# A mixed-attention block on one core: the order of its interleaved part written by a model of the engines

## The chip, the cores and the metric

The kernel runs on one core of a Trainium2 chip. The metric is the device time of one execution in microseconds. The core has a matmul engine (TensorE, PE in the profile, with its weight loads as PEld), three engines for the other arithmetic (VectorE = DVE, ScalarE = ACT, GpSimd = POOL), and a queue for transfers (SyncE = SP).

## The reference

One layer over 512 tokens of width 1024. A normed and modulated `h` is projected by `w_in` to some 8,450 columns, which feed three branches of eight heads of width 64 each, and three gates. Cut to what matters:

```
h = rms_norm(x) * norm1_g * (1 + sc1) + sh1        # sc, sh, gt from silu(c) @ w_ada
y_fox  = softmax attention with a decay, causal, q and k rms-normed per head
y_hgrn = gated linear recurrence in chunks of 64
y_rwkv = delta-rule recurrence in chunks of 64, then a group norm
merged = sigmoid(g0) * (y_fox @ w_branch[0]) + sigmoid(g1) * (y_hgrn @ w_branch[1]) + sigmoid(g2) * (y_rwkv @ w_branch[2])
x = x + gt1 * (merged @ w_out)
h = rms_norm(x) * norm2_g * (1 + sc2) + sh2
u = conv3(h @ w_up);  x = x + gt2 * ((silu(u_gate) * u_val) @ w_down)
```

All is fp32. A large product is made as three matmuls in a faster fp32 form, from a high and a low part of each operand (`mm3`).

## The kernel before

The kernel has four stages: a start that loads and norms `x` (to 47 us), an interleaved part (47 to about 707 us), the output projection with the second norm, and the feed-forward half (from about 760 us), which is one long run of large matmuls.

In the interleaved part the kernel's Python writes the instructions of seven streams, each a generator: `rwkv_b`, `rwkv_a`, `hgrn` and the attention stream `fox` (each over four pairs of heads), `prep`, `ada_stream` (the rest of the adaLN product, on VectorE), and `big`. `big` is the list of large jobs: the projections from `w_in`, the gates, and the merges with `w_branch`; it writes groups of three large matmuls and asks for the weights of later jobs in `ahead()`, as long as fewer than four halves of weights stand behind the job under way. A half is 256 KB; it comes into one of three `raw` buffers (`load`, line 338) and is split into `whi` and `wlo` (lines 330 and 331), with six buffers each. A weight half thus waits for TensorE to be done with an older one.

The other streams work on a pair of heads in many short steps: small matmuls on tiles of the array (64x64, 32x32, 128x64 and so on), transposes and sums over a head (whole 128x128, and 128x32), with VectorE, ScalarE and GpSimd work between. The matmul results of these streams rotate through five accumulators (tag `br`, `PSB`), those of `big` through three (tag `mm`, `PSM`). Nearly all other tiles share one ring of 62 buffers (`T2`).

A stream gives control back with `yield`. `run` keeps a clock of TensorE alone (`clk`, advanced by `mm` and `transpose`); a step that yields x is taken up again after 0.9x + 1.65 us of that clock, and of the streams that are due, the first in the list goes. `big` is last, so large matmuls fill what the others leave. `need` waits for a result of another stream, which `post` puts up with a guessed latency. The compiler then builds the queue of each engine from what is written, the earlier written first among those that it holds to be ready.

Of the kernel before, what the change touches and what calls it, by code (L numbers as in the profile page):

```python
# [40 lines left out]

@with_exitstack
def block_kernel(ctx: ExitStack, tc: tile.TileContext, I, out, dbg=None, upto=99):
    nc = tc.nc
    sync, v, s, g, pe = nc.sync, nc.vector, nc.scalar, nc.gpsimd, nc.tensor
# [18 lines left out]
    LAT = (0.9, 1.65)  # L64
# [15 lines left out]
    clk = [0.0]  # L80

    def mm(o, lhsT, rhs, start=True, stop=True):
        n = rhs.free_size() if hasattr(rhs, "free_size") else math.prod(rhs.shape[1:])
        if rhs.dtype == F32R:
            clk[0] += n / 2400
        else:
            half = (0.5 if lhsT.shape[0] <= 64 else 1.0) * (0.25 if math.prod(lhsT.shape[1:]) <= 32 else 1.0)
            clk[0] += half * max(0.17, n / 600)
        return pe.matmul(o, lhsT=lhsT, rhs=rhs, start=start, stop=stop)  # L89

    def transpose(o, i, idn):
        clk[0] += 0.11 if i.shape[0] > 64 else 0.07
        pe.transpose(o, i, idn)
# [15 lines left out]
    def run(streams):  # L109

        live = [[gen, 0.0, False] for gen in streams]
        while live:
            done = False
            for st in live:
                if st[1] > clk[0] + 1e-9:
                    continue
                c0, n0 = clk[0], len(avail)
                try:
                    lat = next(st[0])
                except StopIteration:  # L120
                    live.remove(st)
                    done = True
                    break
                if lat is None and c0 == clk[0] and n0 == len(avail):
                    continue
                lat = lat or 0.0
                st[1] = clk[0] + (lat * LAT[0] + LAT[1] if lat else 0.0)
                done = True
                break
            if not done:  # L130
                later = [st[1] for st in live if st[1] > clk[0] + 1e-9]
                assert later, "streams wait for each other"
                clk[0] = min(later)

    def PSM():
        return psm.tile([P, 512], F32, tag="mm", name=nm("mm"))

    def PSB():
        return psb.tile([P, 512], F32, tag="br", name=nm("br"))
# [186 lines left out]
    def split(raw, shape, leng):  # L326
        hi = wp.tile(list(shape), F32R, tag="whi", bufs=WB[1], name=nm("whi"))
        lo = wp.tile(list(shape), F32R, tag="wlo", bufs=WB[2], name=nm("wlo"))
# [5 lines left out]
    def load(src, r0, nr, c0, ncol):  # L334
        nld[0] += 1
        sh = [P, nr // P, ncol]
        raw = wp.tile(sh, F32, tag="raw", bufs=WB[0], name=nm("raw"))
# [111 lines left out]
    def head_sums(sqs, sums=None):  # L449
# [8 lines left out]
        yield 0.6  # L458
# [24 lines left out]
    def hgrn(gi):  # L483
# [10 lines left out]
        yield 3.5  # L494
# [9 lines left out]
        yield 1.5  # L504

        fa = T2("fta")
        for li, m in enumerate(LEVELS):
# [28 lines left out]
            yield 2.0  # L536
# [16 lines left out]
        yield 1.8  # L553
# [12 lines left out]
        yield 3.0  # L566
# [7 lines left out]
        yield 1.0  # L574
# [3 lines left out]
        yield 1.0  # L578
        on = T2("on", [P, 8, 64])
        v.tensor_tensor(out=on, in0=as3(ps, 64), in1=bc(ss, 2, [P, 8, 64]), op=ALU.mult)  # L580
        yield 1.0
# [4 lines left out]
        yield 0.8  # L586
        dump("yh", y, lambda d: d[gi * P:(gi + 1) * P, :])
        post(("y", 1, gi), y, 0.0)

    def hgrn_evac(n, gi, ps):  # L590
# [13 lines left out]
        post((n, gi), t, 1.5)  # L604
# [9 lines left out]
    def fox_decay():  # L614
# [8 lines left out]
        yield 6.0  # L623
# [6 lines left out]
        yield 1.5  # L630
        s.activation(nz, nz, AF.Exp)
        s.activation(nz, nz, AF.Ln, bias=1.0)
        yield 2.0
# [14 lines left out]
        yield 0.0  # L648

    def fox_evac(n, gi, ps):  # L650
        raw = T2(n)
        s.activation(raw, ps, AF.Copy)
        post((n, gi), raw, 1.0)

    def fox(gi):
# [5 lines left out]
        yield 1.2  # L661
# [13 lines left out]
        yield 5.0  # L675
        for qi in range(2):
            rnx = head_spread(rn[:, qi, :])
            yield 0.8
# [14 lines left out]
            yield 0.0  # L693
# [6 lines left out]
        yield 3.0  # L700
        y = T2("yf")
        for tt in range(4):
# [14 lines left out]
            yield 1.0  # L717
# [5 lines left out]
            yield 1.0  # L723
# [4 lines left out]
            yield 1.0  # L728
# [10 lines left out]
            yield 1.0  # L739
# [6 lines left out]
            yield 0.0  # L746
# [696 lines left out]
```

## Time and profile before

| | |
|---|---|
| median of 3 runs | 1132.48 us (1131.71 to 1133.53) |
| profiled execution | 1132.57 us, span 1130.7 us |
| TensorE busy | 1072.1 us, 95% of the span |
| VectorE, ScalarE, GpSimd busy | 677.5, 525.8, 277.1 us |
| mean granted TensorE clock | 0.985 of 2.4 GHz |

The span is what lies between the first and the last instruction. Busy times come from the profiler's records; matmuls overlap in the array, so their mean durations (0.39 us for a large one) are longer than their spacing (0.23 us).

### The profile page before, as it was taken

Reading aid. Unit: us, or ns where it says so; the run is one execution under the profiler, and the core shown is the slowest. Engines: PE = TensorE matmul, PEld = TensorE weight load, DVE = VectorE, ACT = ScalarE, POOL = GpSimd, SP = SyncE. Lnnn points to the kernel's source line nnn. Section 1 sums busy time; section 2 is a strip of 40 time slices with the busy share of each in tenths; the row PEclk is TensorE's granted clock in tenths of the full one; section 3 lists DMA queues with packets and bytes.
Section 4 is the critical chain, followed back from the end, with each engine's and each line's share of the span. In section 5 each row is a group of like instructions: output and inputs, shape, how many; then the busy total and the mean of one; then the engine's idle time right before and its main releaser. Section 6 shows DMA issues by size and latency. Waiting matters only on the chain. (4 is left out here: it accounts for less than half of the span.)

```text
span 1130.7 us, 19788 instructions
## 1 busy us (share of the span) xinstructions
PE 1072.1 (95%) x7617; PEld 856.0 (76%) x7617; DVE 677.5 (60%) x1369; ACT 525.8 (47%) x967; POOL 277.1 (25%) x274
## 2 busy tenths in 40 slices
PE   4988999899999999989999999899999999999998
PEld 2567777778777777767778887678888888888886
DVE  2567666777688776786744617446666656651124
ACT  3475475366556647386444235124444444442220
POOL 4015421414341341340022514332011110101100
PEclk9999999899999999999999999899999999999999
DMA  9623233214422441344335365202333333332232
GB/s 323 199 72 86 72 91 95 65 51 134 103 57 73 117 114 49 87 117 127 92 106 175 104 184 170 66 2 71 100 96 100 93 96 101 99 97 95 93 103 84
DMA packets 175476, 117.55 MB, mean 104 GB/s; under 512 B 25360, under 2 KB 151350, under 8 KB 175382
## 3 DMA queue, kind: packets, MB, share of 16 engines
q1 hardware_dynamic: 173696, 116.13, 35.6%
q8 instruction: 60, 0.98, 0.4%
q10 hardware_dynamic: 1238, 0.12, 0.1%
q14 instruction: 34, 0.28, 0.1%
q0 software_dynamic: 448, 0.03, 0.0%
HBM read 112.49 MB, written 3.77 MB: 103 GB/s over the span
## 5 line engine op out<-in xcount | busy, mean ns | idle before, releaser
L330 ACT ACTIVATE whi<-raw 128x512 fp32r<-128x512 f32 x282 | 176.6, 630 | 342.8 <-PE mm L89 227.8
L331 DVE TENSOR_TENSOR wlo<-raw,whi 128x512 fp32r<-128x512 f32 x212 | 151.5, 715 | 152.1 <-ACT whi L330 151.7
L331 POOL TENSOR_TENSOR wlo<-raw,whi 128x512 fp32r<-128x512 f32 x70 | 94.0, 1342 | 516.9 <-ACT whi L330 503.7
L89 PE MATMUL mm<-hhi,whi 128*128 128x512 f32 x504 | 205.2, 407 | 2.8 <-ACT gt L1095 2.5
L89 PE MATMUL mm<-hhi,wlo 128*128 128x512 f32 x504 | 198.8, 394 | 0.0
L89 PE MATMUL mm<-hlo,whi 128*128 128x512 f32 x504 | 198.6, 394 | 0.0
L89 PE MATMUL mm<-h2hlo,whi 128*128 128x512 f32 (+1 forms) x376 | 141.5, 377 | 1.2 <-POOL h2hlo L1293 1.2
L89 PE MATMUL mm<-h2hhi,whi 128*128 128x512 f32 (+1 forms) x376 | 141.3, 376 | 0.0
L89 PE MATMUL mm<-h2hhi,wlo 128*128 128x512 f32 (+1 forms) x376 | 141.2, 376 | 0.0
L89 PEld LDWEIGHTS mm<-hhi,whi 128*128 128x128 f32 x504 | 95.5, 189 | 25.0 <-ACT gt L1095 2.9
L89 PEld LDWEIGHTS mm<-hhi,wlo 128*128 128x128 f32 x504 | 95.2, 189 | 20.9 <-issue 0.4
L89 PEld LDWEIGHTS mm<-hlo,whi 128*128 128x128 f32 x504 | 95.6, 190 | 18.2 <-issue 0.8
L89 PEld LDWEIGHTS mm<-h2hlo,whi 128*128 128x128 f32 x376 | 70.7, 188 | 14.8 <-POOL h2hlo L1293 2.0
L89 PEld LDWEIGHTS mm<-h2hhi,wlo 128*128 128x128 f32 x376 | 70.7, 188 | 12.9
L89 PEld LDWEIGHTS mm<-h2hhi,whi 128*128 128x128 f32 x376 | 70.7, 188 | 12.8
L1351 DVE SCALAR_TENSOR_TENSOR u<-mm,cw,u 128x511 f32<-128x511 f32 x44 | 32.9, 747 | 54.6 <-ACT u L1350 54.6
L1171 DVE SCALAR_TENSOR_TENSOR adac<-ada,cs,adac 128x512 f32<-128x512 f32 x56 | 45.7, 816 | 10.7 <-DMA ada<-in_w_ada_dram 10.6
L89 PE MATMUL br<-wlo,ahi 128*128 128x512 f32 x110 | 42.8, 389 | 0.0
L89 PE MATMUL br<-whi,alo 128*128 128x512 f32 x110 | 42.8, 389 | 0.0
L89 PE MATMUL br<-whi,ahi 128*128 128x512 f32 x110 | 42.8, 389 | 0.0
L89 PE MATMUL mm<-yhi,whi 128*128 128x512 f32 x96 | 38.3, 399 | 0.0
L89 PE MATMUL mm<-yhi,wlo 128*128 128x512 f32 x96 | 37.5, 390 | 0.0
(387 smaller groups left out, 1936.9 us busy)
## 6 DMA issues: line engine op xcount, KB each, us to landing
raw<-in_w_in_dram SPq DMA_DIRECT2D x126, 256.0 KB
ada<-in_w_ada_dram SPq DMA_DIRECT2D x96, 256.0 KB
raw<-in_w_up_dram SPq DMA_DIRECT2D x88, 256.0 KB
raw<-in_w_down_dram SPq DMA_DIRECT2D x44, 256.0 KB
raw<-in_w_branch_dram SPq DMA_DIRECT2D x24, 256.0 KB
wo<-in_w_out_dram SPq DMA_DIRECT2D x16, 256.0 KB
x<-in_x_dram SPq DMA_DIRECT2D x8, 256.0 KB
mg<-in_x_dram SPq DMA_DIRECT2D x8, 256.0 KB
```

The costliest lines, as they stand in the source:

```text
L89: return pe.matmul(o, lhsT=lhsT, rhs=rhs, start=start, stop=stop)
L330: s.activation(hi, raw, AF.Copy)
L331: (g if leng == "g" else v).tensor_tensor(out=lo, in0=raw, in1=hi.bitcast(F32), op=ALU.subtract)
L1171: v.scalar_tensor_tensor(out=acc, in0=raws[n], scalar=cs[:, k:k + 1], in1=acc, op0=ALU.mult, op1=ALU.add)
L1351: v.scalar_tensor_tensor(out=u[:, 1:], in0=ps[:, :511], scalar=cw[:, 1, jj:jj + 1], in1=u[:, 1:], op0=ALU.mult, op1=ALU.add)
```

## The change

`run` no longer goes by a clock of TensorE and fixed latencies. A new class `Plan` keeps a model of all engines while the Python writes: each engine's operations with an estimated cost, when each tile is ready and when it was last used, the slots of accumulators and of weights, the transfers, and in which tile shape TensorE works. `v`, `s`, `g` and `sync` become `Planned` objects, which pass every call on and enter it in the model. A step now says of what kind its next work is: `"f"` (free: goes first whenever ready), `"s"` (small tiles), `"b"` (large). Small steps are held while whole matmuls run, until 3 us have passed since the last return to whole ones or since the step was ready. The constants were not changed elsewhere: `WB`, `NP2` and the loop `ahead()` are as before. Two steps are cut: `split2` of `rk` and of the adaLN sums is now followed by a `yield` before the matmuls that read it. One more `yield` stands before the `BK` transposes.

```diff
+SEM, DRAIN, CHANGE, ENTER = 0.08, 0.2, 0.11, 0.1
+START, HOLD, SLACK = 47.0, 3.0, 0.1
+class Plan:
...
+    def place(self, engine, at, took):
+        b = self.busy.setdefault(engine, [])
...
+        for i, (x, y) in enumerate(b):
+            if at + took <= x:
+                b.insert(i, (at, at + took))
+                return at + took
+            at = max(at, y)
+        b.append((at, at + took))
+        return at + took
+
+    def other(self, engine, op, outs, ins):
+        n = outs[0].free_size()
+        psum = any("PSUM" in str(a.space) or "PS" == str(a.space).split(".")[-1] for a in (*outs, *ins))
+        if engine == "ACT":
+            took = 0.2 + 0.85e-3 * n + (0.19 if len(outs) > 1 else 0.0)
+        elif engine == "POOL":
+            took = 0.3 + 2.2e-3 * n if n > 16 else 0.2 + 0.18 * n
+        else:
+            one = len([a for a in ins if a.free_size() > 8]) < 2 and not psum
+            took = 0.17 + (0.6e-3 if one else 1.15e-3) * n + (0.08 if psum else 0.0)
+        end = self.place(engine, max(self.when((*outs, *ins)), self.slot.get(outs[0].tensor.name, 0.0)) + SEM, took)
+        self.done(outs, ins, end)
+        self.seg = max(self.seg, end)
+
+    def transfer(self, o, i):
...
+        self.sp = max(self.sp, self.when((o, i)), self.slot.get(o.tensor.name, 0.0)) + 0.1
+        self.dma = max(self.sp, self.dma) + 4 * n / 250e3
+        self.done([o], [i], self.dma + 2.0)
+
+    def matmul(self, o, w, x, turn=False):
...
+        at = max(self.pe, self.when((w, x)) + SEM, self.slot.get(o.tensor.name, 0.0) + SEM)
+        if mode != self.mode:
+            at += CHANGE + (ENTER if mode == WHOLE else 0.0)
+            self.mode = mode
+        self.pe = at + took
+        self.done([o], [w, x], self.pe + DRAIN)
...
-    def need(*keys):
+    def need(*keys, kind="f"):
         for k in keys:
             while k not in avail:
                 yield None
-        t = max(avail[k][0] for k in keys) - clk[0]
-        if t > 0:
-            yield t
+        yield (kind, max(avail[k][0] for k in keys))
         return [avail[k][1] for k in keys]
-    def post(key, val, lat=0.0):
-        avail[key] = (clk[0] + lat, val)
+    def post(key, val):
+        avail[key] = (plan.seg, val)
     def run(streams):
-        live = [[gen, 0.0, False] for gen in streams]
...
-                lat = lat or 0.0
-                st[1] = clk[0] + (lat * LAT[0] + LAT[1] if lat else 0.0)
...
+        plan.begin(START)
+        live = [dict(gen=gen, at=plan.pe, kind="f", n=-1, big=i == len(streams) - 1) for i, gen in enumerate(streams)]
+        left = plan.pe
         while live:
+            t = plan.pe
+            ready = [st for st in live if st["n"] != len(avail) and st["at"] <= t + SLACK]
+            small = [st for st in ready if st["kind"] == "s"]
+            free = [st for st in ready if st["kind"] == "f" and not st["big"]]
+            big = [st for st in ready if st["big"]]
+            if plan.whole() and big and small and t - left < HOLD and t - min(st["at"] for st in small) < HOLD:
+                small = []
+            pick = free or small or big
+            if not pick:
...
+                plan.pe = max(plan.pe, min(st["at"] for st in later))
+                continue
...
+            if plan.whole() and not was:
+                left = plan.pe
...
+            elif isinstance(y, float):
+                st["kind"], st["at"] = "f", plan.pe + y
+            elif y == "b":
+                st["kind"], st["at"] = "b", plan.wready
+            else:
+                st["kind"], st["at"] = y, plan.seg
...
@@ def hgrn
-        yield 3.5
+        yield "f"
...
-            yield 2.0
+            yield "s" if m < 32 else "f"
...
@@ def rwkv_a
+        yield "f"
+        parts = split2(rk)
+        yield "f"
         psk = PSB()
-        for i, part in enumerate(split2(rk)):
+        for i, part in enumerate(parts):
             mm(psk, bones, part, i == 0, i == 1)
...
@@ def rwkv_b
-            yield 0.4
+            yield "s"
...
@@ def ada_stream
+                parts = split2(acc)
+                yield "f"
                 ps = PSB()
-                for i, part in enumerate(split2(acc)):
+                for i, part in enumerate(parts):
                     mm(ps, onesr, part, i == 0, i == 1)
...
@@ def big
             cur = queue[0]
-            yield from cur[0][1](cur[1])
+            w = cur[1]
+            plan.wready = plan.when(w[0]) if isinstance(w, list) else 0.0
+            yield "b"
+            plan.wready = 0.0
+            yield from cur[0][1](w)
             queue.pop(0)
-            yield 0.0
+            yield "b"
```

## Rows read from the trace of the kernel before

**Rows 1.** The page, part 1: busy time, share of span and instructions.

```profile
PE 1072.1 (95%) x7617; PEld 856.0 (76%) x7617; DVE 677.5 (60%) x1369; ACT 525.8 (47%) x967; POOL 277.1 (25%) x274
```

**Rows 2.** Windows: length, busy PE, PEld, DVE, ACT, POOL, clock, DMA share, GB/s.

```profile
47.00:600.00 553.00, 524.02 (x5118) 413.03 (x5117) 394.95 (x939) 317.89 (x608) 164.00 (x162) 0.98 0.34 91
600.00:707.00 107.00, 104.06 (x458) 85.33 (x456) 56.66 (x68) 42.93 (x75) 38.67 (x26) 1.00 0.52 155
```

**Rows 3.** TensorE's waits, 47 to 600 us: total us, times, longest.

```profile
PE br L93 <- DVE L L727: 7.5, 4, 4.4
PE br L93 <- DVE rnx L439: 3.4, 3, 1.9
PE br L89 <- POOL pr L493: 3.0, 1, 3.0
PE br L89 <- DVE ST L1035: 3.0, 3, 1.4
PE mm L89 <- ACT gt L1095: 2.5, 1, 2.5
PE br L89 <- DVE slo L467: 2.2, 3, 1.4
PE br L89 <- ACT shi L466: 1.3, 1, 1.3
PE br L93 <- DVE gxc L1064: 1.1, 2, 0.6
```

**Rows 4.** ScalarE's waits, 47 to 600 us.

```profile
ACT whi L330 <- PE mm L89: 89.7, 48, 5.3
...
ACT whi L330 <- DMA raw<-in_w_in_dram: 8.9, 6, 2.3
```

**Rows 5.** The tile adac: nanoseconds at least, median, at most.

```profile
L1171 DVE SCALAR_TENSOR_TENSOR adac<-ada,cs,adac x56: 731/745/1780, 169.8 to 624.7; 128x512 f32<-128x512 f32 x56
```

**Rows 6.** Groups by line: busy us, mean ns, idle before.

```profile
L721 ACT ACT_TABLE_LOAD x14 | 18.0, 1283 | 4.1 <-DVE nmx L715 3.9
```

**Rows 7.** Timeline of ScalarE at a table load.

```profile
201.69 1.28 ACT L721 ACT_TABLE_LOAD   x1
202.98 0.62 ACT L721 ACTIVATE L<-L,nmx 128x384 f32<-128x384 f32 x1
```

**Rows 8.** Timeline of TensorE around one run of small tiles.

```profile
119.39 0.39 PE L89 MATMUL mm<-hlo,whi 128*128 128x512 f32 x1
119.61 0.39 PE L89 MATMUL mm<-hhi,wlo 128*128 128x512 f32 x1
119.93 1.12 PE L89 MATMUL br<-hq,kt 64*64 64x32 f32 x32
120.98 0.50 PE L89 MATMUL mm<-hhi,whi 128*128 128x512 f32 x1
121.32 0.39 PE L89 MATMUL mm<-hlo,whi 128*128 128x512 f32 x1
```

**Rows 9.** Timeline of TensorE: one short stretch of whole matmuls.

```profile
204.79 0.33 PE L89 MATMUL br<-ST,MT 64*64 64x64 f32 x4
205.05 0.50 PE L89 MATMUL mm<-hhi,whi 128*128 128x512 f32 x1
...
208.00 0.33 PE L89 MATMUL br<-ST,MT 64*64 64x64 f32 x4
```

**Rows 10.** Windows with a granted clock below 1, columns as in rows 2.

```profile
100.00:150.00 50.00, 49.28 (x471) 39.41 (x470) 30.94 (x74) 26.29 (x53) 16.50 (x21) 0.97 0.30 72
...
200.00:250.00 50.00, 44.47 (x495) 36.70 (x494) 38.55 (x94) 25.12 (x57) 16.44 (x20) 0.90 0.21 55
...
500.00:550.00 50.00, 47.46 (x436) 37.19 (x434) 34.10 (x77) 31.66 (x62) 7.07 (x6) 0.97 0.43 123
```

**Rows 11.** Timeline of TensorE: the two matmuls that sum `rk`.

```profile
106.92 0.50 PE L89 MATMUL br<-shi,bonesr 128*128 128x512 f32 x1
...
108.15 0.51 PE L89 MATMUL br<-slo,bonesr 128*128 128x512 f32 x1
```

More of the change, by code (lines that the diff above doesn't have):

```diff
@@ new lines, with __init__, __getattr__, call @@
+class Planned:
+    def __init__(self, engine, name, plan):
+        self.engine, self.name, self.plan = engine, name, plan
+    def __getattr__(self, op):
+        f = getattr(self.engine, op)
+        def call(*args, **named):
+            aps = [a for a in args if hasattr(a, "tensor")]
+            outs = [named[k] for k in ("out", "accum_out") if named.get(k) is not None]
+            if "out" not in named:
+                outs, aps = [aps[0], *outs], aps[1:]
+            ins = aps + [a for k, a in named.items() if k not in ("out", "accum_out") and hasattr(a, "tensor")]
+            if op == "dma_start":
+                self.plan.transfer(outs[0], ins[0])
+            else:
+                self.plan.other(self.name, op, outs, ins)
+            return f(*args, **named)
+        return call
@@ L76, in small @@
         return bp.tile(list(shape), F32, tag="sm_" + n, bufs=bufs, name=nm(n))
-    clk = [0.0]
+    plan = Plan()
+    v, s, g, sync = (Planned(e, n, plan) for e, n in ((nc.vector, "DVE"), (nc.scalar, "ACT"), (nc.gpsimd, "POOL"), (nc.sync, "SP")))
     def mm(o, lhsT, rhs, start=True, stop=True):
[L83 to L88, printed above, removed]
+        plan.matmul(o, lhsT, rhs)
         return pe.matmul(o, lhsT=lhsT, rhs=rhs, start=start, stop=stop)
     def transpose(o, i, idn):
-        clk[0] += 0.11 if i.shape[0] > 64 else 0.07
-        pe.transpose(o, i, idn)
+        plan.matmul(o, i, idn, True)
+        return pe.transpose(o, i, idn)
     avail = {}
-    def need(*keys):
+    def need(*keys, kind="f"):
         for k in keys:
@@ new lines, in run @@
+            if plan.whole() and big and small and t - left < HOLD and t - min(st["at"] for st in small) < HOLD:
+                small = []
+            pick = free or small or big
+            if not pick:
+                later = [st for st in live if st["n"] != len(avail)]
+                assert later, "streams wait for each other"
+                plan.pe = max(plan.pe, min(st["at"] for st in later))
+                continue
+            st = pick[0]
+            was = plan.whole()
+            plan.seg, p0, n0 = 0.0, plan.pe, len(avail)
@@ new lines, in run @@
+            try:
+                y = next(st["gen"])
+            except StopIteration:
+                live.remove(st)
+                continue
+            if plan.whole() and not was:
+                left = plan.pe
+            st["n"] = -1
+            if y is None:
+                st["n"] = n0
+            elif isinstance(y, tuple):
+                st["kind"], st["at"] = y
+            elif isinstance(y, float):
+                st["kind"], st["at"] = "f", plan.pe + y
+            elif y == "b":
+                st["kind"], st["at"] = "b", plan.wready
+            else:
+                st["kind"], st["at"] = y, plan.seg
@@ L805, in rwkv_evac @@
                 ll.append(st)
-            t, lat = ll, 5.0
-        post((n, j % 4 if j < 12 else 0), t, lat)
+            t = ll
+        post((n, j % 4 if j < 12 else 0), t)
     def f2(ap):
@@ L1006, in rwkv_a @@
                 s.activation(UV[HS[hh], hf * 4:hf * 4 + 4, hh, :], pv[HS[hh], :, 1, :], AF.Copy)
-        post(("A", gi), (G, AR, UV, W, wc, bv), 1.2)
-        yield 0.0
+        post(("A", gi), (G, AR, UV, W, wc, bv))
+        yield "f"
     def rwkv_b(gi):
         gs = slice(gi * P, (gi + 1) * P)
-        (G, AR, UV, W, wc, bv), = yield from need(("A", gi))
+        (G, AR, UV, W, wc, bv), = yield from need(("A", gi), kind="s")
         MT = T2("MT", [P, 8, 64])
@@ L1088, in compute @@
                 mm3(ps, w[k][0], w[k][1], hhi[:, k, :], hlo[:, k, :], k == 0, k == 7)
-                yield 0.0
+                plan.wready = plan.when(w[(k + 1) % 8])
+                yield "b"
             evac(*arg, ps)
```

204 lines of the change are left out of this document (117 added, 87 removed).

## The prediction, made before the changed kernel ran

> **What bounds the kernel now.** I read the page's busy times first, then the windows of the interleaved part, then the list of what TensorE waited for there, and last the timeline around some of those waits. The page says that TensorE is busy for 95% of the span while VectorE stands at 60% and ScalarE at 47% [rows 1]. So the kernel is a long TensorE queue, and a new order of writing can win three things only: TensorE's idle time, time lost at the lower clock, and time lost in switching between whole 128x128 matmuls and small tiles of the array. The matmuls themselves are the same before and after.
>
> The interleaved part reaches from 47 us to about 707 us. From 47 to 600 us, TensorE is busy for 524.02 of 553.00 us, so 28.98 us are idle [rows 2]. From 600 to 707 us it is busy for 104.06 of 107 us [rows 2]: only large matmuls are left there, so the small streams have some 100 us of slack and their length does not set the end. What stands behind 707 us (the output projection and all after it) is written as before, and I leave it unchanged.
>
> The waits of the 553 us are short and scattered [rows 3]: 7.5 us for the scaled softmax rows `L`, 3.4 us for `rnx`, 3.0 us for `pr`, 3.0 us for `ST`, 2.5 us for `gt` (a large matmul that wants its accumulator back), 2.2 and 1.3 us for `slo` and `shi`, and eight lesser ones, from `gxc` with 1.1 us down, 5.2 us together. None is for a transfer: ScalarE waited 89.7 us with a weight half in hand until TensorE freed its slot, and 8.9 us for a transfer [rows 4]. Weights are far enough ahead.
>
> **The change, part by part.**
>
> *Weights four halves ahead.* The diff leaves the loop `ahead()` and the numbers of buffers untouched; before, it already fetched until four halves stood behind the current job. Cost and gain: nothing. What hides the transfers is the slot wait of [rows 4]; with that cover gone the price is at least the 8.9 us already seen.
>
> *Two steps cut in two.* `split2` of `rk` and of the adaLN sums used to be written in the same step as the matmuls that read it, so these stood at the head of the queue while ScalarE and VectorE were still at it. Now a step ends between them. That takes away 2.2 + 1.3 = 3.5 us [rows 3]; large matmuls fill the place.
>
> *Ready times from a model in place of guessed latencies.* Before, a step that yields x was held for 0.9x + 1.65 us of the planner's clock, so each had 1.65 us of margin. Now it is released when the model says that its operands are done, give or take a tenth of a microsecond. The model knows the engines' queues, the accumulators' slots and a cost for each operation. Of the listed waits, such a model can see `pr` 3.0, `ST` 3.0, `gt` 2.5 and the eight lesser ones 5.2: 13.7 us. With the 3.5 us above, 17.2 us of the 28.98 go. I keep the remaining 11.8 us, `L` and `rnx` above all: they wait for VectorE, the longest of them 4.4 us [rows 3], and VectorE's times scatter in a way that the model does not have. The same `adac` operation takes 731 ns at best, 745 in the median and 1780 at worst [rows 5], where the model always books 0.76 us.
>
> The margin also covered what the model leaves out. ScalarE loads a table 14 times in front of the softmax exponentials, 18.0 us at 1283 ns each [rows 6], and the model books none. Each makes a scaled `L` late by 1.28 us, and the transposes of `L` are released at once. Bounds: nothing, if other work stands ahead of each, to 18.0 us, if TensorE meets all of it. TensorE takes up a step only after the group of three large matmuls under way, 0.7 us at a spacing of 0.23 us, which eats half of a delay, and not every load lies on such a path: I take a third, 6 us of new waits. Net of this part with the two splits: 17.2 - 6 = 11 us gained.
>
> A load is followed at once by its activation (the load at 201.69 us, the exponential at 202.98 us), so a change of tables costs 1.29 us here [rows 7]. The Trainium skill (ScalarE: Activation LUTs, "What ACT_TABLE_LOAD costs") puts it at about 2.66 us, with a drain of some 1.38 us beside the load; the trace shows the load and no drain. By the page's figure the unbooked time would be 14 x 2.66 = 37 us (an estimate), a third of it 12 us, and the net of this part 5 us in place of 11.
>
> *Small matmuls are held back up to 3 us while whole ones run.* One excursion costs 0.20 us: at 119.61 us the last large matmul starts, 0.32 us later the small ones, against 0.23 between large ones; and the first large one behind them is followed after 0.34 us [rows 8]. So 0.09 + 0.11. I counted the timeline from 47 to 600 us: TensorE comes back to whole matmuls 92 times, and 53 of these stretches are shorter than 3 us. Fourteen hold only transposes and other small whole matmuls, which the new rule still lets in at once; 39 hold large ones. Thirteen of the 39 last 2.94 to 2.99 us, as the one from 205.05 to 208.00 us between two steps of the `ST` chain [rows 9]; a limit of 3 us barely moves them. That leaves 26: 26 x 0.20 = 5 us. Bounds: 0 and 39 x 0.20 = 8 us.
>
> *Clock.* After three long waits TensorE ran at its lower level, 1.2 GHz, for a while. The loss, length times what is missing in the granted clock, is 50 x 0.03, 50 x 0.10 and 50 x 0.03 us [rows 10], 8.0 us in all. The first (1.5 us) follows the wait for `pr`, which goes. The others follow waits for `L`, which I let stay in part; a third of 6.5 us is 2.2 us. Gain 4 us, bounds 0 and 8.
>
> *More in the step rules.* `need` now always ends a step, and the adaLN stream pauses 3.0 us where it paused 0.9 x 3.0 + 1.65 = 4.35; VectorE is at 38.55 of 50 us where the longest wait lies [rows 10], so there is little room for more. I put no gain on it; its loss is in the second rival.
>
> Sum: 11 + 5 + 4 = 20 us. The profiled execution took 1132.57 us around a span of 1130.70, and the median of the runs is 1132.48, so one stands for the other: 1132.5 - 20 = 1112.5 us.
>
> **The rivals.**
>
> *Nearly all waits go.* The compiler orders each queue by its own idea of what is ready: the matmul on `slo` is written straight behind that on `shi`, and the trace has 1.2 us of other matmuls between them [rows 11]. If that mends what the model leaves out, idle time falls by 22 to 29 us, the clock returns 6 to 8 and the switches 5 to 8: 33 to 45 us, 1087 to 1099 us. Against it: in the kernel before the same compiler let the 4.4 us through.
>
> *Late data, slower.* Steps released without margin meet data that come later than booked. The code has 26 steps with TensorE work of the kind that goes first per head, 104 over four heads. If each waits 0.3 us (one stretched VectorE operation is late by up to 1.0 [rows 5], a table load by 1.28 [rows 6]), that is 31 us of new idle time in place of my 6; the sum turns from -20 to +5, and with the clock lost again rather than won to about +10: 1143 us. It decides from 0.25 us per step, where new waits reach 26 us and eat all of 17.2 + 5 + 4. For it: VectorE's 77% and the unbooked times. Against it: a step is picked only between groups, so half a group, 0.35 us, is margin on average, and the held small steps have up to 3 us.
>
> *Waits move.* The queue's order is the compiler's in the end [rows 11]; old waits go, as many others come, and only the switches are saved: 1127 to 1134 us.
>
> **How the numbers follow.** The forecast (1099 to 1127 us, its own range) gets 0.48, nearly all waits gone 0.12, waits moved 0.15, late data 0.25. A difference of 0.2%, 2.3 us, is about what a measurement tells from none. Of the third case half lies below 1130.2 us, nearly all else within 2.3 us of the old time. Faster: 0.48 + 0.12 + 0.07 = 0.67; the same 0.08; slower 0.25. The range leaves out the best half of the second case and the worse half of late data: 1092 to 1138 us.
>
> **What would show it.** In the windows from 47 us to the end of the small streams: TensorE idle near 18 us against 28.98; no waits for `shi`, `slo` and `pr`; returns to whole matmuls near 65 against 92; a granted clock of 1.00 from 100 to 150 us; waits for `L` still there, most of them behind a table load or a stretched VectorE operation. The stretch from about 707 us on should be the same, only earlier. The prediction is wrong if idle time in this part stays at 29 us or grows, above all in front of transposes and head sums, or if the number of switches does not fall; and it is too careful if the waits for `L` and `rnx` vanish as well.

## The result and the profile after

The changed kernel takes 1142.86 us in the median of 8 runs (1137.91 to 1148.48), the kernel before 1133.28 us in the runs beside them: a ratio of 1.0083, with a 95% interval of 1.0064 to 1.0102. It is slower by 0.8%, where 1.8% faster was forecast, and above the range. Its executions scatter over 10.6 us, those of before over 3.7 us.

The profiled execution after took 1139.66 us, 7.1 us more than that of before. The page's busy times of the kernel after, which answer to [rows 1]:

```profile
span 1137.9 us, 19793 instructions
PE 1079.6 (95%) x7617; PEld 859.2 (76%) x7617; DVE 668.6 (59%) x1369; ACT 525.0 (46%) x966; POOL 276.8 (24%) x274
```

TensorE has as many matmuls as before, and is busy 7.5 us longer with them. Windows of the kernel after, with the columns of [rows 2]:

```profile
47.00:600.00 553.00, 523.80 (x5088) 409.44 (x5087) 396.01 (x947) 317.30 (x607) 163.61 (x161) 0.98 0.34 93
600.00:707.00 107.00, 107.00 (x474) 88.60 (x473) 40.48 (x55) 38.68 (x68) 33.42 (x23) 1.00 0.48 141
100.00:150.00 50.00, 44.98 (x429) 35.71 (x430) 28.13 (x70) 22.14 (x47) 17.43 (x22) 0.86 0.31 73
200.00:250.00 50.00, 43.04 (x492) 34.07 (x492) 40.55 (x94) 22.31 (x44) 16.34 (x23) 1.00 0.37 102
500.00:550.00 50.00, 49.97 (x482) 40.12 (x483) 27.27 (x82) 36.72 (x70) 8.38 (x7) 1.00 0.30 80
```

Idle time from 47 to 600 us is 553.00 - 523.80 = 29.20 us, against 28.98 in [rows 2]; 11 us less was forecast. The clock from 200 to 250 and from 500 to 550 us is whole, which [rows 10] had at 0.90 and 0.97; but from 100 to 150 us it is 0.86, where [rows 10] had 0.97. The first matmul of the output projection starts at 710.49 us, before at 703.20 us; what lies behind it lasts 427.4 us now and 427.5 us before. So all 7.3 us are lost in the interleaved part.

TensorE's waits of the kernel after, 47 to 600 us, columns as in [rows 3] (helpers now record the lines):

```profile
PE br L209 <- POOL pr L163: 6.1, 3, 4.9
PE br L213 <- DVE rnx L163: 4.8, 5, 1.9
PE br L213 <- DVE gxc L163: 4.8, 3, 2.8
PE br L213 <- DVE on L163: 2.4, 2, 2.0
PE br L213 <- DVE hs L163: 1.9, 1, 1.9
PE br L209 <- ACT fp L163: 1.8, 1, 1.8
PE br L209 <- POOL AR L163: 1.6, 1, 1.6
PE br L209 <- DVE ri L163: 1.6, 1, 1.6
PE br L213 <- DVE L L163: 1.2, 1, 1.2
PE br L209 <- DVE kt L163: 0.9, 1, 0.9
PE br L209 <- DVE slo L163: 0.6, 1, 0.6
PE br L209 <- ACT shi L163: 0.3, 1, 0.3
```

The old waits did go: `L` from 7.5 to 1.2 us, `ST` 3.0 and `gt` 2.5 us entirely, `slo` from 2.2 to 0.6 us and `shi` from 1.3 to 0.3 us, 14.4 us in all. Others came for them: `pr` 3.1 us more, `gxc` 3.7, `rnx` 1.4, and `on`, `hs`, `fp`, `AR`, `ri` and lesser ones 11.2 us, where the lesser ones of before without `gxc` had 4.7. That is 14.7 us of new waits for 14.4 us of old ones.

What came can be followed at the longest, `pr` at 104.43 us. The timelines of TensorE, VectorE, ScalarE, GpSimd and SyncE in the kernel after; the bracket is the idle time before an instruction and what ended it:

```profile
99.12 0.39 PE L209 MATMUL mm<-hlo,whi 128*128 128x512 f32 x1
104.43 0.65 PE L209 MATMUL br<-pr,con 128*32 128x128 f32 x8 [4.92 <-POOL pr L163]
...
96.23 0.53 DVE L163 TENSOR_SCALAR gate<-sig,omlb,lb 128x512 f32<-128x512 f32 x1
101.67 0.69 DVE L163 TENSOR_TENSOR wlo<-raw,whi 128x512 fp32r<-128x512 f32 x1 [4.91 <-ACT whi L163]
102.28 0.42 DVE L163 TENSOR_SCALAR ft<-gate 128x512 f32<-128x512 f32 x1
102.62 0.42 DVE L163 TENSOR_SCALAR kt<-gate 128x512 f32<-128x512 f32 x1
...
101.01 0.63 ACT L163 ACTIVATE whi<-raw 128x512 fp32r<-128x512 f32 x1 [7.82 <-DMA raw<-in_w_in_dram]
...
96.38 1.51 POOL L163 TENSOR_TENSOR wlo<-raw,whi 128x512 fp32r<-128x512 f32 x1
103.12 1.26 POOL L163 TENSOR_TENSOR pr<-hq,kt 128x512 f32<-128x512 f32 x1 [5.22 <-DVE kt L163]
...
97.92 4.84 SPq L163 DMA_DIRECT2D raw<-in_w_in_dram  x4
```

Read it backwards. TensorE waits for `pr`; GpSimd makes `pr` from `kt`; `kt` reads `gate`, done at 96.76 us, but stands in VectorE's queue behind a `wlo`, which waits 4.91 us for its `whi`; ScalarE waits 7.82 us for a weight transfer, issued at 97.92 us, when GpSimd had freed the `raw` buffer. An operation with its operands in hand stands five microseconds behind one without. The planner could not see it: its `place` puts an operation into any hole of an engine's future, as if `kt` could pass `wlo`. The Trainium skill (TensorE: Matmul & The Clock Gate, "Architectural detail: the array is 16× 32×32, not 1× 128×128") says that VectorE's and ScalarE's queues are strictly first in, first out; these rows agree, `kt` starts 0.95 us after the `wlo` that had waited.

Not all long waits are of this kind. The second longest, 2.75 us for `gxc`, stands behind GpSimd:

```profile
235.98 0.69 DVE L163 TENSOR_TENSOR gxc<-gxc,gvar 128x512 f32<-128x512 f32 x1 [2.72 <-POOL gvar L163]
...
234.31 1.64 POOL L163 TENSOR_TENSOR gvar<-gvar,neghalf 128x8 f32<-128x8 f32 x1
```

VectorE had written its `gvar` by 232.62 us; GpSimd worked on other operations until 234.3 us and then took 1.64 us for it.

That transfer also answers the forecast's first point. ScalarE's waits of the kernel after, as in [rows 4]:

```profile
ACT whi L163 <- PE mm L209: 62.9, 38, 5.2
ACT whi L163 <- DMA raw<-in_w_in_dram: 29.1, 10, 7.8
```

The wait for transfers grew from 8.9 to 29.1 us.

### The profile page after: what moved, and what is told of

It reads as the page before. It is cut to its first block, busy times and chain, and to the rows that moved or that the text cites. A ratio compares the mean times of both kernels' runs of the same rounds, so it can differ in the third digit from the quotient of the medians.

```text
span 1137.9 us, 19793 instructions
## 1 busy us (share of the span) xinstructions
PE 1079.6 (95%) x7617; PEld 859.2 (76%) x7617; DVE 668.6 (59%) x1369; ACT 525.0 (46%) x966; POOL 276.8 (24%) x274
## 5 line engine op out<-in xcount | busy, mean ns | idle before, releaser
L163 DVE SCALAR_TENSOR_TENSOR u<-mm,cw,u 128x511 f32<-128x511 f32 x88 | 65.8, 748 | 56.2 <-ACT u L163 54.7
L209 PEld LDWEIGHTS mm<-h2hhi,wlo 128*128 128x128 f32 x376 | 70.7, 188 | 12.7
L163 DVE SCALAR_TENSOR_TENSOR adac<-ada,cs,adac 128x512 f32<-128x512 f32 x56 | 46.6, 833 | 10.2 <-DMA ada<-in_w_ada_dram 10.0
```

The costliest lines, as they stand in the source:

```text
L163: return f(*args, **named)
```

## The experiments

All ratios are against the kernel before, in runs beside it. The columns: ratio with its interval; granted clock, the median of all runs; time x clock, the median of each run's product, an estimate of what an order would need at the whole clock (it treats waits as if they shrank too); idle from 47 to 600 us, by windows of the profiled execution; and the returns to whole matmuls from 47 us to the output projection, counted in its timeline (91 for before, where the prediction counted 92). The last column is the time that the `AR,BK` products take, from the start of each run of them to the next instruction, less idle. One execution of each kernel was profiled, so the last three columns have no interval, and the execution need not be a typical one: that of raw4 took 9.9 us and that of t_hold6 12.2 us more than the median of the kernel's runs, that of b_splits 5.3 and that of cap3 5.7 us less.

| kernel | ratio [95%] | clock | time x clock | idle | returns | AR,BK (runs) |
|---|---|---|---|---|---|---|
| before | 1 | 0.986 | 1116 to 1117 | 28.98 | 91 | 13.3 (6) |
| after | 1.0083 [1.0064, 1.0102] | 0.984 | 1123.7 | 29.20 | 102 | 19.6 (17) |
| gloop | 1.0057 [1.0037, 1.0077] | 0.982 | 1118.5 | 29.89 | 99 | 14.3 (4) |
| margin | 1.0289 [1.0262, 1.0315] | 0.970 | 1131.3 | 36.37 | 111 | 18.4 (16) |
| raw4 | 1.0108 [1.0078, 1.0139] | 0.985 | 1127.4 | 28.36 | 105 | 21.5 (17) |
| b_splits | 1.0057 [1.0037, 1.0078] | 0.983 | 1120.1 | 25.81 | 112 | 12.7 (6) |
| kept_pe | 1.0478 [1.0452, 1.0505] | 0.960 | 1139.9 | 52.42 | 95 | 18.9 (16) |
| hold0 | 1.0066 [1.0047, 1.0085] | 0.982 | 1119.2 | 27.78 | 123 | 11.1 (4) |
| tables | 1.0040 [1.0025, 1.0054] | 0.977 | 1111.2 | 23.88 | 102 | 18.2 (4) |
| a_tables | 1.0139 [1.0115, 1.0163] | 0.982 | 1127.8 | 30.23 | 98 | 18.5 (17) |
| t_slackm05 | 1.0082 [1.0060, 1.0104] | 0.982 | 1121.8 | 26.65 | 110 | 18.2 (15) |
| lite | 1.0053 [1.0033, 1.0073] | 0.984 | 1119.9 | 28.37 | 103 | 18.5 (17) |
| b_gcut | 1.0133 [1.0108, 1.0157] | 0.979 | 1122.4 | 25.09 | 116 | 20.4 (16) |
| b_lat150 | 1.0066 [1.0041, 1.0091] | 0.988 | 1124.6 | 28.56 | 110 | 12.6 (6) |
| b_lat160 | 1.0041 [1.0027, 1.0056] | 0.981 | 1116.0 | 27.81 | 99 | 12.7 (7) |
| b_lat180 | 1.0153 [1.0129, 1.0176] | 0.977 | 1125.1 | 33.99 | 106 | 13.9 (8) |
| t_sem | 1.0030 [1.0019, 1.0042] | 0.980 | 1113.9 | 29.62 | 94 | 15.8 (5) |
| t_hold6 | 1.0086 [1.0067, 1.0105] | 0.981 | 1119.9 | 36.77 | 91 | 16.0 (5) |
| cap3 | 1.0026 [1.0009, 1.0043] | 0.980 | 1115.4 | 26.75 | 98 | 14.1 (4) |
| ts_cap3 | 1.0170 [1.0147, 1.0192] | 0.970 | 1117.6 | 34.64 | 99 | 15.4 (4) |

### The cut G loop: gloop and b_gcut

The diff also turned a `yield 0.0` of `rwkv_a` into `yield "s"`. The four groups of eight `AR,BK` products of a head, which do not need each other, used to be written one behind the other; now each waits in the plan until the group before it has been taken out of its accumulator.

*gloop*, the changed kernel with this undone:

```diff
 v.tensor_tensor(out=G[hh][hf], in0=as3(ps, 128), in1=bc(K(f"gmask{hh}"), 1, [P, 4, P]), op=ALU.mult)
-                yield "s"
+                yield 0.0
```

> The changed kernel with one step rule of before put back: the four products of the G loop follow each other at once, instead of each being held until the evacuation of the one before is done by the model. Theory A (the loop was cut by its own rule: 8 matmuls per excursion instead of 16 or 32): the 64x128 products of AR and BK take about 13 us instead of 19.6, TensorE returns to whole matmuls some 91 times instead of 102, and the time falls by some 6 us, ratio to before about 1.003. Theories B (data later than the model books) and C (weight halves late): no change, ratio 1.008, idle time about 29 us in the interleaved part under all three.

*b_gcut*, the kernel before with the same loop cut by its own rule (0.9 x 0.1 + 1.65 = 1.74 us of its clock between two groups), and nothing else:

```diff
-                yield 0.0
+                yield 0.1
```

> The kernel before with one edit of the change alone: the products of the G loop are cut apart (yield 0.1 in place of yield 0.0, so some 1.7 us of other work comes between them). Theory (the cut costs by the switches and the lone runs of 8): AR,BK takes some 5 us more than the 13.3 us of before, some 8 to 12 more returns; ratio 1.004 to 1.008. Rival (the cut keeps stretches of small products short and so wins clock; what it costs is given back): ratio 0.998 to 1.002, clock above 0.987.

The cut alone makes the kernel before slower by 1.3%, more than the whole change does; undoing it in the changed kernel gives back 4.2 us of the median (1138.71 us), though the two intervals overlap. The timelines of TensorE show its price: in the kernel before

```profile
93.29 2.82 PE L89 MATMUL br<-AR,BK 64*128 64x128 f32 x32
```

and in b_gcut

```profile
365.12 1.16 PE L89 MATMUL br<-AR,BK 64*128 64x128 f32 x8
366.20 0.97 PE L89 MATMUL br<-ST,AR 64*64 64x64 f32 x15
```

Eight take 1.08 us by themselves and 0.70 us as a quarter of 32. In b_gcut they take 20.4 - 13.3 = 7.1 us more in all, and there are 272 changes of tile shape in place of 234, at 0.1 us (the 0.09 and 0.11 us of [rows 8]) 3.8 us; 3.9 us of idle time were won; and the clock fell from 0.986 to 0.979, worth about 0.007 x 1140 = 8 us. That is 15 us, and the median is 15.6 us above that of before. It is a rough sum: some of the lower clock and of the changes of shape lies within the 7.1 us. The theory's sign held, and its size (1.004 to 1.008) was too small by what the clock took.

### Are the waits those of the model's margin, of the transfers, of VectorE, of TensorE's queue?

*margin*, the changed kernel with the old margin put back on each modelled ready time:

```diff
-        yield (kind, max(avail[k][0] for k in keys))
+        yield (kind, max(avail[k][0] for k in keys) + MARGIN)    # 1.65
...
-                st["kind"], st["at"] = y, plan.seg
+                st["kind"], st["at"] = y, plan.seg + MARGIN
```

> The changed kernel with the old margin of 1.65 us added to every modelled ready time of a step and of a posted result. Theory B: idle time in the interleaved part falls from 28.9 to 15 us or less, and the time by 10 us or more, ratio to before 0.998 or less. Theory A: AR,BK still stand in 17 runs, idle time may fall a little, ratio 1.005 to 1.008. Theory C: the waits behind late weights stay (pr above all), idle time 22 us or more, ratio 1.003 to 1.008.

*raw4*, with a fourth `raw` buffer (two constants' tiles moved into the ring to make room):

```diff
-    WB = (3, 6, 6)
+    WB = (4, 6, 6)
```

> The changed kernel with a fourth buffer for weights as they come from memory (two small tiles of the start move into the common ring to make room). Theory C: ScalarE's waits for weight transfers fall from 29.1 us to 10 or less, the 4.9 us wait for pr falls below 2, idle time by 6 us or more, ratio to before about 1.002. Theories A and B: transfers may come earlier but TensorE's idle time stays near 29 us, ratio 1.007 to 1.009.

*lite*, the planned order as it is, with less work on VectorE; it leaves out 7/8 of the columns in 56 of the adaLN products:

```diff
-                v.scalar_tensor_tensor(out=acc, in0=raws[n], scalar=cs[:, k:k + 1], in1=acc, ...)
+                plan.other("DVE", "scalar_tensor_tensor", [acc], [raws[n], cs[:, k:k + 1], acc])
+                nc.vector.scalar_tensor_tensor(out=acc[:, :64], in0=raws[n][:, :64], scalar=cs[:, k:k + 1], in1=acc[:, :64], ...)
```

> The changed kernel with its written order as planned, but 56 operations of VectorE on the adaLN sums work on 64 of 512 columns, so that part of the adaLN products is left out; the model still books them in full. VectorE has some 35 us less to do. Theory V (the waits that the model did not foresee come from VectorE's queue being full and stretched): idle falls from 28.9 to below 22 us, ratio 0.998 to 1.003. Rival (they come from the order of the queues, not from the load): idle 26 to 31 us, ratio 1.005 to 1.010.

*kept_pe*, the changed kernel with every matmul of the part ordered behind the one written before it:

```diff
+    q = sorted(plan.queue["PE"], key=lambda x: x[:2])
+    for (_, _, a), (_, _, b) in zip(q, q[1:]):
+        tc.add_manual_dep(b, a.name, ..., reason="planned order")
```

> The changed kernel, with TensorE's queue tied to the written order (each matmul of the interleaved part is ordered behind the one written before it), while the compiler still builds the queues of VectorE, ScalarE and GpSimd as it likes. Theory D (the waits that the model did not foresee come from the compiler's departures from the planned order on TensorE): idle falls from 28.9 to below 22 us, ratio 1.000 to 1.003. Rival 1 (the departures are on the other three queues, or the times differ from the model): idle stays at 27 to 32 us, ratio 1.007 to 1.010. Rival 2 (the compiler's departures mend waits): idle grows by 5 us and more, ratio above 1.012.

None of the four theories held. With the margin put back, idle time grew to 36.4 us and the clock fell to 0.970: releasing the steps later by the old margin does not cure the waits. With a fourth buffer ScalarE's wait for transfers to `whi` fell from 29.1 to 2.0 us, as these rows of raw4 show, and TensorE's longest wait for `pr` from 4.9 to 3.2 us:

```profile
ACT whi L163 <- DMA raw<-in_w_in_dram: 2.0, 2, 1.6
PE br L209 <- POOL pr L163: 3.2, 1, 3.2
```

yet idle time stayed at 28.4 us: the wait that the transfer caused was replaced by others. With 25.7 us less work for VectorE in these operations (46.6 to 20.9 us in the groups by line; some 35 us was expected) idle time stayed near where it was, 28.4 us, and the kernel was still 0.5% slower than before. And with TensorE's queue as written, idle time rose to 52.4 us; the head of its list of waits, 47 to 720 us:

```profile
PE br L226 <- DVE rnx L170: 12.0, 4, 4.5
PE br L219 <- ACT shi L170: 5.7, 4, 2.3
PE br L226 <- DVE gxc L170: 4.2, 3, 2.4
```

So the compiler's departures from the written order of TensorE do not make the waits. Without them idle time is some 23 us longer, as the prediction's first rival thought possible, and the plan as it is written for TensorE is worse than what ran. Tying the other three queues to the plan was not tried.

### What the model leaves out: tables, and what follows from it

*tables*, gloop with ScalarE's table loads in the model; t_slackm05, a step of it counts as ready 0.5 us after the model's time; a_tables, the same model with the G loop cut as in the change:

```diff
+    table = {AF.Exp: "e", AF.Ln: "e", AF.Sigmoid: "s", AF.Tanh: "s"}.get(func) if engine == "ACT" else None
...
+            load = 1.28 if table and now and now != table else 0.0
+            back = 1.28 if table and q and q != table and now != table else 0.0
+            if max(at, end) + load + took + back <= x:
...
-START, HOLD, SLACK = 47.0, 3.0, 0.1       # t_slackm05 only
+START, HOLD, SLACK = 47.0, 3.0, -0.5
```

> The kernel gloop whose model also books 1.28 us for each change of ScalarE's function tables (30 changes in its plan; the trace of the changed kernel has 36 loads in the part). Theory E (the new waits come from times that the model leaves out, table loads first): steps behind a load are released later, other matmuls fill the place, idle falls from gloop's 29.5 to 20 to 25 us, ratio 0.997 to 1.001. Rival (the waits come from the order of the queues that the compiler builds, not from unbooked times): idle 27 to 32 us, ratio 1.004 to 1.009.

> The kernel tables in which a step counts as ready only 0.5 us after the model's time (0.1 us before it, until now); its own model books 2.4 us of idle in place of 9.9. Theory E2 (what is left of waits comes from steps taken up a few tenths too early): idle below 18 us, clock above 0.982, ratio 0.992 to 1.000. Rival (as margin showed: later steps only move the waits along the chains): idle 22 to 30 us, ratio 1.003 to 1.012.

> The changed kernel whose model books ScalarE's table loads, as in tables, but with the products of the G loop cut apart as in the changed kernel (17 runs of 8). In tables the idle time fell to 23.75 us while the granted clock fell to 0.977: after a wait of 1.8 us for ST a stretch of 13 us of small products ran at the lower clock. Theory K (a wait followed by a long stretch of small products is what loses the clock; short stretches lose less): idle 22 to 26 us, granted clock back at 0.983 to 0.987, no stretch of small tiles over 6 us, ratio 0.998 to 1.004. Rival (the lower clock of tables came with its waits, wherever small products stand): clock 0.976 to 0.980, and the cut costs 4 to 6 us besides: ratio 1.007 to 1.010.

With the loads booked, idle time fell from gloop's 29.89 to 23.88 us, in the range that theory E gave. That the booking did it is not shown. The other planned orders that book the loads had 26.65 us (t_slackm05), 26.75 (cap3), 29.62 (t_sem), 30.23 (a_tables), 34.64 (ts_cap3) and 36.77 us (t_hold6), and t_sem differs from tables by 0.02 us in one constant. The windows of gloop, tables and t_sem, in this order:

```profile
47.00:600.00 553.00, 523.11 (x5087) 409.25 (x5086) 392.27 (x947) 316.07 (x605) 167.82 (x161) 0.98 0.35 93
47.00:600.00 553.00, 529.12 (x5101) 417.56 (x5100) 397.78 (x947) 316.88 (x607) 171.07 (x162) 0.96 0.35 94
47.00:600.00 553.00, 523.38 (x5090) 412.62 (x5089) 402.99 (x946) 312.91 (x603) 168.45 (x161) 0.97 0.34 93
```

The time of tables is 1.0040, where gloop has 1.0057 and an interval that overlaps; its granted clock went down to 0.977. By the product of time and clock this order would need 1111 us, 5 us less than that of before. By windows of 10 us from 50 to 700 us tables loses 20.7 us to the lower clock (length times what is missing), before and after 8.5 us each. A window of tables (columns as in [rows 2]) and TensorE's timeline show one of the four places where it does:

```profile
458.00:468.00 10.00, 10.00 (x98) 9.54 (x99) 8.56 (x26) 5.44 (x12) 1.27 (x1) 0.50 0.23 55
```

```profile
457.91 0.48 PE L215 MATMUL br<-ST,MT 64*64 64x64 f32 x4 [1.78 <-DVE ST L169]
458.32 5.13 PE L215 MATMUL br<-AR,BK 64*128 64x128 f32 x32
463.38 1.44 PE L215 MATMUL br<-VM,ktok 64*64 64x64 f32 x22
...
467.32 3.31 PE L215 MATMUL br<-UV,G 128*64 128x64 f32 x32
470.56 0.47 PE L215 MATMUL br<-VM,A 64*64 64x64 f32 x2
470.96 0.76 PE L215 MATMUL mm<-hhi,whi 128*128 128x512 f32 x1
471.55 0.40 PE L215 MATMUL mm<-hlo,whi 128*128 128x512 f32 x1
471.79 0.40 PE L215 MATMUL mm<-hhi,wlo 128*128 128x512 f32 x1
```

After a wait of 1.78 us for `ST` the clock is at 0.50, its level of 1.2 GHz, and stays there while TensorE is busy for all of ten microseconds with small tiles: the 32 products take 5.13 us, where the kernel before did 32 in 2.82 us. The later margin of t_slackm05 took off nothing more (26.65 us), and a_tables showed that shorter stretches of small tiles do not bring the gain either: its clock came back to 0.982, its waits to 30.2 us.

### How much holding saves: hold0 and t_hold6

```diff
-START, HOLD, SLACK = 47.0, 3.0, 0.1
+START, HOLD, SLACK = 47.0, 0.0, 0.1      # hold0, on gloop; 6.0 in t_hold6, on tables
```

> The kernel gloop (independent products of the G loop written without a wait between them) with a holding time of 0 in place of 3 us: small steps are no longer held back while whole matmuls run. Its own model books 253 changes of tile shape in place of 231 and an end that is 7.8 us later. If holding saves switches as the prediction said (0.2 us for each return), some 10 more returns than gloop's 99 and 2 to 4 us more: ratio 1.007 to 1.010. Rival (holding delays the chains of the small streams and costs as much in waits as it saves in switches): ratio 1.003 to 1.006, idle below gloop's 29.5 us.

> The kernel tables with a holding time of 6 in place of 3 us; its own model books 204 changes of tile shape in place of 228 and an end at 703.1 in place of 693.7 us. If switches are what is left: some 12 returns fewer than the 102 of tables, 2 to 3 us won, 1.001 to 1.003. Rival (held steps come late and bring waits, as the model books): idle above 27 us, 1.006 to 1.012.

Without holding there are 123 returns in place of gloop's 99: 24 x 0.20 = 4.8 us more for switching, and the median is 1.3 us longer (1140.05 against 1138.71 us, intervals that overlap); 2.1 us less idle time is a part of what pays for it. With 6 us there are 91 returns, and idle time is 36.8 us in place of 23.9. Holding does save switches; that it saves time is not shown, and at 6 us the profiled execution has 12.9 us more of waits.

### Is it the planned order, or any other order: b_splits, b_lat150, b_lat160, b_lat180, t_sem

*b_splits* is the kernel before with the two cut steps of the change alone:

```diff
+        parts = split2(rk)
+        yield 1.0
...
-        for i, part in enumerate(split2(rk)):
+        for i, part in enumerate(parts):
```

and the same for the adaLN sums.

> The kernel before with one part of the change alone: split2 of rk and of the adaLN sums stands in a step of its own, followed by the old rule's pause of 2.55 us. By the prediction's term the waits for shi and slo (3.5 us) go and nothing takes their place: ratio 0.997. Rival (waits move: whatever is next in the queue waits instead): waits for shi and slo gone, idle time still 27 to 30 us, ratio 0.999 to 1.001.

The three *b_lat* kernels move before's own margin a little; *t_sem* moves one constant of tables, `SEM`, from 0.08 to 0.10:

```diff
-    LAT = (0.9, 1.65)
+    LAT = (0.9, 1.5)          # 1.6 in b_lat160, 1.8 in b_lat180
```

> The kernel before with one constant of its planner changed: the margin of a step is 1.5 us in place of 1.65 us, so that streams are taken up a little earlier and the order of writing changes here and there; nothing else is touched. Theory F (the order of before is a lucky or tuned one among many alike, and most other orders leave other waits of about the same sum and a few more switches): slower by 0.2 to 0.8%, ratio 1.002 to 1.008, TensorE's idle time from 47 us to the output projection within 25 to 33 us. Rival (before's rule is robust, and the changed kernel is slower for something in its model): ratio 0.998 to 1.002, idle 28 to 29 us.

> The kernel before with a margin of 1.60 in place of 1.65 us, nothing else. Theory F (before's order is a picked one among many alike): 1.002 to 1.010, with idle time of 24 to 32 us and more switches or a lower clock. Rival (before's rule is robust, b_lat150 was an exception): 0.998 to 1.002.

> The kernel before with a margin of 1.80 in place of 1.65 us, nothing else. Theory F: 1.002 to 1.010. Rival: 0.998 to 1.002.

> The kernel tables (ratio 1.0040) with the model's time from one engine to another at 0.10 in place of 0.08 us, nothing else; its own model books an end at 698.1 in place of 693.7 us. Theory F: planned orders scatter by several tenths of a per cent whatever their model says, so anything from 1.002 to 1.012. Rival (the model's account tells): 4 us more than tables, 1.007 to 1.009.

b_splits did what it was meant to: the waits for `shi` and `slo` went, idle time fell by 3.2 us where the prediction had 3.5. But the order came out with 112 returns in place of 91, the clock at 0.983, and the kernel 0.6% slower. And a margin moved by 0.05 to 0.15 us, with nothing else changed, costs 0.4, 0.7 and 1.5%. The three lose it in three ways: b_lat160 in the clock alone (its product of time and clock is that of before), b_lat150 with the highest clock of all, at 110 returns, and b_lat180 in waits and clock. The order of before is better than each of its five neighbours that ran (these four and b_gcut). How it came to be the better one no run shows. The planned orders scatter as well: t_sem, for which the model books 4 us more than for tables, took as long as tables (1.0030).

### A rule for the clock: cap3 and ts_cap3

```diff
+            if not plan.whole() and big and t - since > CAP:     # 3.0
+                pick = big
+            else:
+                pick = free or small or big
```

> The kernel tables with one more rule: when TensorE has worked on small tiles for 3 us of the model's time and a large step is ready, the large step goes. Theory C2 (long stretches of small products hold the clock down once it has fallen): no stretch of small tiles over 6 us, granted clock 0.983 to 0.987 in place of 0.977, idle 22 to 27 us, ratio 0.995 to 1.000, faster than before. Rival (the waits make the clock fall and the order is another draw): clock 0.976 to 0.982, ratio 1.003 to 1.010.

> The kernel t_sem (ratio 1.0030, clock 0.980) with the same rule. Theory C2: clock 0.983 to 0.987, ratio 0.996 to 1.001. Rival: clock 0.976 to 0.982, ratio 1.002 to 1.010.

The rule failed. In cap3 the longest stretch of small tiles is 5.0 us, but the clock is 0.980 in the median; in ts_cap3, where other waits made stretches of 8.3 us again, it is 0.970. cap3 has the lowest ratio of the planned orders, 1.0026 [1.0009, 1.0043], next to t_sem with 1.0030, and does not beat the kernel before. Twelve executions of this one program took 1130.94 to 1139.50 us; the three up to 1132.80 us had a granted clock of 0.982 to 0.986, the three from 1138.85 us on 0.980. The clock does not settle the time alone: the lowest, 0.978, belongs to 1136.68 us, the middle of the twelve. In its profiled execution, 1130.94 us, the output projection starts at 700.84 us, 2.4 us earlier than in that of before.

## Why the prediction was wrong, step by step

*Weights, priced at nothing*: the edit is indeed none, but its cover was not safe. The new order turned the wait for transfers from 8.9 to 29.1 us, and one such wait stands behind the 4.9 us for `pr`. Taking it away (raw4) bought nothing, so the price in the end was near nothing, for another reason than the one given.

*17.2 us of waits go*: right in part. Of these, 10.9 us went: `ST`, `gt`, most of `slo` and `shi`, and some of the lesser ones. `pr`, `gxc`, `hs` and `fp`, which were counted in too, grew; `pr` doubled. `L`, which I had let stay, lost 6.3 us, so the total of the waits that shrank is near the forecast by luck. (The lesser ones of before are nine and come to 5.5 us, not eight and 5.2.)

*6 us of new waits*: this is the step that failed first. Some 15 us came, and idle time stayed at 29.20 us. I had sized them by the table loads alone. Even these I had undercounted: ScalarE's timeline from 47 us to the output projection has 37 loads before and 36 after, not the 14 in front of the exponentials. But in the four longest waits of the kernel after (`pr`, `gxc`, `on`, `hs`) the last load had ended 6 us or more before TensorE went on, and the 6.0 us that tables won is no more than what planned orders differ by. The longest wait, `pr` behind `wlo`, comes from a queue in which a ready operation stands behind one that is not, where the model lets it pass; `gxc` waits for a busy GpSimd. What makes the rest stays open.

*Holding, 26 returns fewer*: the sign of the sum was wrong; the count went from 91 to 102. Holding alone does save 24 returns (gloop against hold0), close to the 26. But I took them off the returns of before's order, and the planned order without holding has 123 (hold0). The cut G loop adds 3 more (102 against gloop's 99) and leaves pieces of eight: I named the steps that were cut in two and missed the one cut in four. In the profiled executions the loss adds up: changes of tile shape went from 234 to 259, 2.5 us; `AR,BK` took 6.3 us more, of which the 0.11 us for leaving each of 11 more pieces is in the changes already, 1.2 us; idle time 0.2 us more from 47 us to the output projection. That is 7.8 us against the 7.3 us by which the projection starts later; it is a rough sum, since the `AR,BK` time holds 1.8 us of lower clock, and that of before some 1.4 us (16 products in 3.02 us at 218.07 us, 16 in 1.64 us at 227.01 us).

*Clock, 4 us gained*: none was. The loss, length times what is missing in the granted clock in stretches of 10 us from 50 to 700 us, is 8.5 us in both profiled executions: the two stretches at `L` were won, and the one from 90 to 120 us, behind waits of 1.6 us for `AR` and 4.9 us for `pr`, grew from 1.7 to 8.5 us. These rows of TensorE's timeline in the kernel after are behind the wait for `pr`:

```profile
105.02 2.07 PE L209 MATMUL br<-AR,BK 64*128 64x128 f32 x8
107.02 0.79 PE L209 MATMUL mm<-hhi,wlo 128*128 128x512 f32 x1
...
110.52 2.07 PE L209 MATMUL br<-AR,BK 64*128 64x128 f32 x8
112.52 0.79 PE L209 MATMUL mm<-hhi,whi 128*128 128x512 f32 x1
```

Two pieces of eight stand at the lower level, 2.0 us each in place of 1.09. In the other executions of the kernel after the clock is lower, 0.984 in the median against 0.987 in the profiled one. That is 0.003 x 1143 = 3.4 us, and the median lies 3.2 us above the profiled execution; before, it lies 0.7 us above. So 7.1 us between the profiled executions become 9.6 us between the medians.

*The rivals*: the mechanism that happened is that of "waits move", whose idle time it has; that case had switches saved and ended at 1127 to 1134 us. The time that happened, 1142.86 us, is that of "late data", whose mechanism did not: waits did not grow by 31 us. That its 1143 us was met is luck. I also gave 0.48 of the chance, the largest share, to a forecast that priced the order of before as if it were an ordinary one. The runs with its constant moved say that it is not: in each of them leaving it cost 0.4 to 1.5%. That the changed kernel started behind by as much is argued from them, not shown.

*What stays open*: why some orders, and some executions of the same order, are granted less clock. tables and t_sem need less than before by time x clock and lose it there. Waits of TensorE stand in front of the stretches that were looked at, but a wait as long need not lower it (from 230 to 250 us, around the 2.75 us for `gxc` in the kernel after, the clock is 1.00), idle time does not rank the kernels by clock (b_gcut 25.1 us of idle and 0.979, before 28.98 and 0.986), and shorter stretches of small tiles did not bring it back.

## What to carry to other kernels

Before you price a new order, move a constant of the old one by a few per cent and measure: if its neighbours are all slower, the old order is better than an ordinary one, and a new one may start behind by that much. Read a diff that changes scheduling for every place where work that stood together is cut apart; here one such `yield`, put into the kernel before, cost 1.3%. A model of the engines is only as good as its queues: one that lets a ready operation pass a waiting one can book too little idle time, as at `pr` here, and a wait removed from its list is not won until the sum of idle time has fallen.

## What the runs showed of the hardware

- Eight 64x128 products by themselves take 1.08 us, 32 in a row 2.82 us, 0.70 us for eight of them: 0.38 us are lost at the edges of a piece.
- At the lower level of the clock the 32 take 5.13 us. TensorE stayed at that level through 10.00 us in which it was busy throughout with small tiles, and the spacing of large matmuls was back at 0.24 us 0.6 us after the first of them. The Trainium skill (TensorE: Matmul & The Clock Gate, "What's actually happening") names two levels, 1.2 and 2.4 GHz; 5.13 against 2.82 us, a factor of 1.8, goes with that.
- The same program, run twelve times, differed by 8.6 us (cap3), and its granted clock went from 0.978 to 0.986; the time follows the clock only in part, since 0.978 came with 1136.68 us and 0.982 with the shortest, 1130.94 us.
